# Another order of the projections in a two-layer hybrid decoder trunk, with later square roots and no forced wait for 1/rms

## The chip, the cores and the metric

One core of one Trainium2 chip runs the whole program. The metric is device microseconds from start to end of one execution. All arithmetic is at float32 precision: each product is formed by three matmuls on operands that are split into a rounded high part and a low rest (hi x hi, hi x lo, lo x hi). Weights stream from HBM once, 1 MB at a time, and are split on the chip.

## The reference

Two layers, 256 positions, width 1024. In each layer:

```
x = x + 0.5 * swiglu(rms_norm(x, ffn1_norm), w_gate, w_up, w_down)          # FFN 1, inner width 2816
h = rms_norm(x, mix_norm)
q, k, v, f, xr, gr, gA, gR = split(h @ w_in + b_in)                         # 1024 columns each, f has 8
q, k = rms_norm per head (8 heads of 128)
y_attn = softmax(q.k/sqrt(d) + c_t - c_s, causal) @ v, then @ w_o_attn      # c = cumsum(log_sigmoid(f))
xr = causal depthwise conv, width 4
r, i = sigmoid(block_diag(xr)), two gates
a = exp(-8 r softplus(-lam));  u = sqrt(1 - a^2) * i * xr;  hs_t = a_t hs_{t-1} + u_t
y_rnn = (hs * gelu(gr)) @ w_o_rnn
x = x + (sigmoid(gA) * y_attn + sigmoid(gR) * y_rnn) @ w_out
x = x + 0.5 * swiglu(rms_norm(x, ffn2_norm), ...)                           # FFN 2
```

## The kernel before

**A list of steps for TensorE.** The program is planned while it is built. `self.steps` is the fixed order of TensorE's work. A step is half of the product with one weight tile: 6 wide matmuls (512 columns, for q, k, v, whose output has positions on the partitions: `rows`) or 12 narrow ones (256 columns, for all others, whose output has channels on the partitions: `columns`). The mixer of a layer (`mix`, L685) begins at step `base`. Counted from there, before the change: q0 k0 v0 q1 k1 v1 are steps 0 to 47 (eight each; 0 and 1 are the first and the last four heads), xr 48 to 63, gr 64 to 79, gA 80 to 95, gR 96 to 111, then the output projections: attention ("ya") 112 to 127, recurrence ("yr") 128 to 143, and `w_out` 144 to 159. The host lays the weights out in the same order (`_weights`, L1164).

**Tasks for the other engines.** What follows a product is a Python generator (`projected`, `qk`, `head`, `recurrence`, `gated`, `stats`, ...). The planner keeps an own clock per engine (`Clock`, with a cost for each instruction, L75) and advances a task when the tile it names would be ready by that clock (`when`, `work`). Each advance puts instructions into the queues of TensorE (PE), ScalarE (ACT), VectorE (DVE), GpSimd (POOL) or SyncE (SP), which run them in order. A task can also hang on a condition of the plan (`must`). `need` advances tasks by force where a step must have their result. Tasks with the label "rnn" stand first in the list; heads and recurrences are background work, put off while ACT or DVE would be over 3.5 us (`ROOM`) ahead of PE by the planner's clock.

**Weights.** `split_half` turns one 128 x 1024 half of a loaded piece into hi (ACT cast) and lo (DVE subtraction). `run` (L397) does it 5 steps ahead at the latest (`LEAD`) and up to 20 (`AHEAD`) when ACT and DVE have room. Places are 8 W tiles, or R tiles while at least 8 of the 21 are idle. R tiles also hold q, k, v, the recurrence's and the gates' arrays.

**1/rms.** x is not normalised before a product. `stats` sums the squares by a matmul, takes the power on POOL, spreads the result over partitions by a second matmul on a diagonal (`sq`), and leaves it in `self.rb`. `projected` scales q, k, v as they leave PSUM; it gets the factor from `rms`, which forces `stats` on. `scaled` does the same for the columns, but waits for `self.rb`.

**Attention.** Four `head` tasks are spawned when k of their group is done; at most three are under way (`FLY`), in order.

**Recurrence.** `on_xr` spawns `recurrence` (L985) for each half of 512 channels: convolution on DVE (12 multiply-adds), gates by block-diagonal matmuls, tanh and exp on ACT, then a product under a root. The roots of both halves are taken together: Sqrt needs another ACT table than Exp, Tanh and Gelu. They wait until both halves have come so far and all heads are done or the step is over `base + 96`. After them come the scans, and `gated`: gelu (ACT, only once the roots are taken), product and split (DVE). yr reads that.

Of the kernel before, what the change touches and what calls it, by code (L numbers as in the profile page):

```python
# [33 lines left out]
OFF = {"q": 0, "k": 1024, "v": 2048, "f": 3072, "xr": 3080, "gr": 4104, "gA": 5128, "gR": 6152}  # L34
PROJ = [("q", 0), ("k", 0), ("v", 0), ("q", 1), ("k", 1), ("v", 1)]

P_G = {"ffn1": 0, "mix": 8, "ffn2": 16}
P_QN, P_KN, P_CW, P_CB, P_BA, P_BX, P_BGA, P_BGM, P_LAM, P_BXR, P_BGR, P_BV, NP_ = 24, 25, 26, 58, 66, 74, 82, 90, 98, 106, 114, 122, 130
LEAD = 5
# [9 lines left out]
AHEAD = 20  # L49
SLACK = 2.0  # L50
EARLYX = -0.4
SIDES = False

AT = 16, 48
# [7 lines left out]
class Clock:  # L62
# [12 lines left out]
    def cost(self, q, op, n, ins, kw):  # L75
        aps = sum(isinstance(kw.get(k), bass.AP) and kw[k].shape[-1] == 1 for k in ("scale", "bias", "scalar", "scalar1", "scalar2"))
        psum = ins and ins[0].space == bass.MemoryType.PSUM
        if q == "PE":
            two = ins[0].dtype == F32 and op == "matmul"
            return 2 * max(2 * n / 2400 + 0.003, 0.06) if two else max(n / 2330 + 0.007, 0.108)  # L80
        if q == "ACT":
            t = (0.051 if psum else 0.093) + 0.093 * (aps + (kw.get("accum_out") is not None)) + n / 1200
            need = self.TABLES.get(kw.get("func"))
            if need and self.table not in need:
                self.table = need[0]
                t += 1.3
            return t
        if q == "DVE":
            fast = op in ("tensor_scalar", "tensor_copy", "memset") and not psum
            return 0.068 + 0.061 * aps + n / (1920 if fast else 960)  # L90
        if q == "POOL":
            return 0.9 + n / 480
        return 0.0
# [103 lines left out]
class Trunk:  # L197
# [199 lines left out]
    def run(self):  # L397
        steps = self.steps
        first, last = {}, {}
        for s, st in enumerate(steps):  # L400
            first.setdefault(st.half, s)
            last[st.half] = s
        n = self.n_halves
        self.loaded, j = 3, 2
        self.first_halves()
        for s, st in enumerate(steps):
            self.s = s
            while j < n and first[j] - s <= LEAD and self.split_places():
                self.split_half(j)
                j += 1  # L410
            self.work()
            while (j < n and first[j] - s <= AHEAD and self.split_places()
                   and self.clock.done[self.raw[j // 2].tensor.name] <= self.now + EARLY
                   and all(self.clock.free[q] <= self.now + SLACK for q in ("ACT", "DVE"))):
                self.split_half(j)
                j += 1
            while st.half not in self.hl:
                if self.split_places():
                    self.split_half(j)
                    j += 1  # L420
                else:
                    self.push()
            hi, lo, places = self.hl[st.half]
            st.fn(hi, lo)
            if last[st.half] == s:
                places.give(hi, lo)
                del self.hl[st.half]
            for gen, label in st.done:
                self.spawn(gen, label)
        while self.tasks:  # L430
            self.push()
# [253 lines left out]
    def mix(self, l):  # L685
        base = len(self.steps)
        phase = self.phase
        self.phase += 1
        M = {"l": l, "p": self.prm_sb[:, l], "base": base, "phase": phase, "heads": 0}
        c = lambda t: slice(t * 128, (t + 1) * 128)  # L690

        def rows(i):

            nm, n = PROJ[i]
            js = [self.half() for _ in range(4)]
            self.spots.update(dict.fromkeys(js, (0, 0)))
            banks = {}

            def step(h, t):
                def fn(wh, wl):  # L700
                    if h == 0:
                        banks[t] = self.take(self.banks)
                    for kk in range(2):
                        k, w = 2 * h + kk, slice(kk * 512, (kk + 1) * 512)
                        xs = self.x_rhs(phase, k)
                        self.mm3(banks[t], xs[:, c(t)], xs[:, 256:512][:, c(t)], wh[:, w], wl[:, w], k == 0, k == 7)
                return Step(js[h], fn, [(self.projected(M, i, t, banks), "v" if nm == "v" else "qk")] if h == 3 else [])
            if i == 0:
                order = [(h, t) for t in range(2) for h in range(3)] + [(3, 0), (3, 1)]
            else:  # L710
                order = [(h, t) for h in range(4) for t in range(2)]
            self.steps += [step(h, t) for h, t in order]

        def columns(ds, rhs, done, late=False):

            banks = {}

            def step(d, half, ks):
                def fn(wh, wl):
                    if ks[0] == 0:  # L720
                        banks[d] = self.take(self.banks)
                    for k in ks:
                        w = slice(k * 128, k * 128 + 128)
                        self.product(banks[d], wh[:, w], wl[:, w], rhs(k), k == 0, k == 7)
                return Step(half, fn, [done(d, banks)] if ks[-1] == 7 else [])
            halves = {d: self.half() for d in ds}
            order = [(d, ks) for d in ds for ks in (range(4), range(4, 8))]
            if late:
                order[0:4] = [(d, ks) for d in ds[:2] for ks in (range(4), range(4, 7))] + [(d, range(7, 8)) for d in ds[:2]]
            self.steps += [step(d, halves[d], ks) for d, ks in order]  # L730

        def y_rhs(k):
            self.need(lambda: M["heads"] > k, "head", "qk", "forget", "v")
            return M["y", k // 2][1][:, k % 2]

        def r_rhs(k):
            self.need(lambda: ("yr", k // 2) in M, "rnn", "gr", "wd", "head")
            return M["yr", k // 2][1][:, k % 2]

        def m_rhs(k):  # L740
            self.need(lambda: ("m", k) in M, "ya", "merge", "gate")
            return M["mT", k // 2][1][:, k % 2]

        for i in range(6):
            rows(i)
        for nm, label, on in (("xr", "rnn", self.on_xr), ("gr", "gr", self.on_gr), ("gA", "gate", self.on_gate), ("gR", "gate", self.on_gate)):
            columns(range(8), lambda k: self.x_rhs(phase, k),
                    lambda d, b, nm=nm, label=label, on=on: (on(M, nm, d, b), label))
        self.starts.append((base - 14, lambda: self.prefetch(M), "bias"))
        self.starts.append((base - 12, lambda: self.block_diagonal(M), "wd"))  # L750
        self.starts.append((base + 8, lambda: self.forget(M), "forget"))
        columns(range(8), y_rhs, lambda d, b: (self.on_ya(M, d, b), "ya"))
        columns(range(8), r_rhs, lambda d, b: (self.on_yr(M, d, b), "merge"))
        columns(list(range(8)), m_rhs, lambda d, b: (self.on_out(M, d, b), "x"), late=True)
# [32 lines left out]

    def block_diagonal(self, M):
        for n in range(2):
            yield self.step_at(M["base"] + (40, 60)[n])  # L790
            raw, w = self.slot([4, 2, 128])
            self.SP.dma_start(out=w, in_=self.wbd[M["l"], n])
            yield self.when(raw, must=lambda: len(self.big.idle) >= 4)
            hi, lo = (self.slot([4, 2, 128], F32R, at) for at in AT)
            self.split(hi[1], lo[1], w)
            self.big.give(raw)
            M["wd", n] = hi, lo

    def projected(self, M, i, t, banks):

        nm, n = PROJ[i]
        bank, r = banks[t], self.rms(M["phase"])[:, t:t + 1]
        if nm == "v":
            if t == 0:
# [180 lines left out]
    def recurrence(self, M, n):  # L985
# [52 lines left out]
        if n == 0:  # L1038
            yield self.when(must=lambda: "roots" in M)
        else:  # L1040
            yield self.when(rt_t, must=lambda: ("rt", 0) in M and (M["heads"] == H or self.s > M["base"] + 96), queues=("ACT",))
            for i in range(2):
                self.ACT.activation(M["rt", i][0], M["rt", i][0], AF.Sqrt, scale=0.25)
            M["roots"] = True
# [119 lines left out]
def _weights(a):  # L1164
    out = []
    for l in range(L):
        w = a["w_in"][l]
        out += _ffn_halves(a["ffn1_w_gate"][l], a["ffn1_w_up"][l], a["ffn1_w_down"][l])
        out += [_rows(w[:, OFF[nm] + 512 * n:OFF[nm] + 512 * n + 512]) for nm, n in PROJ]
        out += [_columns(w[:, OFF[nm]:OFF[nm] + 1024]) for nm in ("xr", "gr", "gA", "gR")]  # L1170
        out += [_columns(a[nm][l]) for nm in ("w_o_attn", "w_o_rnn", "w_out")]
        out += _ffn_halves(a["ffn2_w_gate"][l], a["ffn2_w_up"][l], a["ffn2_w_down"][l])
    w = np.concatenate(out, axis=0)
# [43 lines left out]
```

## Time and profile before

| | |
|---|---|
| median of 3 runs | 1244.05 us (1242.8 to 1245.28) |
| profiled execution: time, span of the trace | 1245.86 us, 1244.1 us |
| PE busy | 1226.0 us, 99% of the span |
| PEld (weight loads of PE) busy | 1194.2 us, 96% |
| DVE busy | 851.8 us, 68% |
| ACT busy | 697.5 us, 56% |
| DMA, mean over the span | 187 GB/s, queue 1 busy 53.0% of 16 engines |
| mean granted TensorE clock | 0.995 |

Busy is time in which an engine has at least one instruction under way; ends of matmuls are modelled. The span runs from the first to the last instruction of the trace and is 1.76 us shorter than the profiled execution's time. All instructions carry line 154, that of the helper which records them, so groups go by tile names: `W` and `R` are the places above, `B` PSUM banks, `S` small tiles, `xs` the split x, `wr` loaded weights, `lg` and `pT` a head's logits and probabilities, `hb`, `prm`, `rst` parameters. In the trace the mixer of layer 0 runs from about 194 to 442 us and that of layer 1 from about 803 us to 1050.

### The profile page before, as it was taken

What the parts mean: (1) busy time and instruction counts of PE and PEld (TensorE: products, weight loads), DVE (VectorE), ACT (ScalarE), POOL (GpSimd) and SP (SyncE); (2) the same over time, 40 slices, a digit from 0 to 9 for tenths busy, and PEclk for the clock granted to TensorE, in tenths of its full rate; (3) what the DMA queues carried; (4) which work ended last, traced back from release to release, by engine and by line L of the source; (5) the groups of instructions that cost most, each with busy time, mean ns of one, the idle gap of its engine ahead of it and who ended that gap; (6) DMA issues with size and microseconds to landing.
All of it is one profiled execution on the core that took longest, in us unless ns stands there. A gap on an engine that the chain in (4) does not pass through costs nothing.

```text
span 1244.1 us, 24052 instructions
## 1 busy us (share of the span) xinstructions
PE 1226.0 (99%) x10040; PEld 1194.2 (96%) x10040; DVE 851.8 (68%) x1411; ACT 697.5 (56%) x1192; POOL 36.0 (3%) x48
## 2 busy tenths in 40 slices
PE   8999999999999999999999999999999899999998
PEld 7999998889999999999999999988999899999998
DVE  6765567678769976565675566776786599665552
ACT  6544446586795664444554445565658746544441
POOL 1000001120000000000000000011100000000000
PEclk9999999999999999999999999999999899999999
DMA  8655566543456755455575455663353557554451
GB/s 296 216 204 171 184 209 243 178 153 119 143 177 213 281 205 172 168 183 187 182 263 183 156 173 200 237 237 139 119 171 124 179 198 249 207 180 169 170 187 52
DMA packets 36029, 232.47 MB, mean 187 GB/s; under 512 B 4528, under 2 KB 5712, under 8 KB 9040
## 3 DMA queue, kind: packets, MB, share of 16 engines
q1 hardware_dynamic: 35776, 230.79, 53.0%
q8 instruction: 79, 1.29, 0.4%
q14 instruction: 30, 0.25, 0.1%
q10 hardware_dynamic: 144, 0.13, 0.0%
HBM read 229.84 MB, written 1.06 MB: 186 GB/s over the span
## 4 chain that ended last, share of the span: by engine, by line
PE 88%; DVE 6%; ACT 2%; DMA 2%; issue 1%; SPq 0%; ACTq 0%; DVEq 0%
PE B L154 88%; DVE R L154 3%; DVE W L154 2%; DMA wr<-ws 2%; ACT R L154 1%; ACT W L154 1%; DMA prm<-prm 0%; ACT L154 0%; SPq L154 0%; DVE acc L154 0%; DVE sq L154 0%; DVE x L154 0%; ACT sq L154 0%; ACT rb L154 0%; ACTq L154 0%
## 5 line engine op out<-in xcount | busy, mean ns | idle before, releaser
L154 DVE TENSOR_TENSOR W<-wr,W 128x1024 fp32r<-128x1024 f32 (+1 forms) x263 | 319.4, 1215 | 221.9 <-ACT W L154 220.4
L154 PE MATMUL B<-xs,W 128*128 128x256 f32 x3480 | 416.6, 279 | 7.1 <-ACT W L154 4.5
L154 PEld LDWEIGHTS B<-xs,W 128*128 128x128 f32 x3480 | 406.6, 189 | 10.0 <-ACT W L154 5.2
L154 ACT CAST W<-wr 128x1024 fp32r<-128x1024 f32 (+1 forms) x263 | 272.4, 1040 | 230.8 <-PE B L154 207.3
L154 PE MATMUL B<-R,W 128*128 128x256 f32 x2304 | 268.3, 277 | 4.3 <-DVE R L154 3.9
L154 PEld LDWEIGHTS B<-R,W 128*128 128x128 f32 x2304 | 265.2, 189 | 4.9 <-DVE R L154 4.3
L154 PE MATMUL B<-xs,R 128*128 128x256 f32 x2280 | 269.0, 277 | 0.0
L154 PEld LDWEIGHTS B<-xs,R 128*128 128x128 f32 x2280 | 263.2, 188 | 0.2
L154 DVE TENSOR_TENSOR R<-wr,R 128x1024 fp32r<-128x1024 f32 x163 | 197.6, 1220 | 66.2 <-ACT R L154 65.8
L154 ACT CAST R<-wr 128x1024 fp32r<-128x1024 f32 x163 | 166.3, 1040 | 3.3 <-DMA wr<-ws 3.2
L154 PE MATMUL B<-R,R 128*128 128x256 f32 (+1 forms) x1024 | 125.9, 279 | 0.0
L154 PEld LDWEIGHTS B<-R,R 128*128 128x128 f32 x1024 | 119.8, 188 | 0.6
L154 ACT ACTIVATE S<-S 128x256 f32<-128x256 f32 x88 | 36.3, 418 | 130.2 <-DVE S L154 130.2
L154 PE MATMUL B<-R,xs 128*128 128x512 f32 x336 | 84.1, 397 | 0.0
L154 PEld LDWEIGHTS B<-R,xs 128*128 128x128 f32 x336 | 61.6, 188 | 12.4
L154 PE MATMUL B<-W,xs 128*128 128x512 f32 x240 | 61.7, 398 | 0.0
L154 ACT CAST R<-S 128x256 fp32r<-128x256 f32 x88 | 34.9, 402 | 38.6 <-DVE S L154 38.6
L154 POOL TENSOR_TENSOR rst<-rst,mhalf 128x4 f32<-128x4 f32 (+1 forms) x22 | 27.2, 1239 | 954.0 <-DVE rst L154 954.0
L154 PEld LDWEIGHTS B<-W,xs 128*128 128x128 f32 x240 | 44.1, 188 | 8.7
L154 DVE TENSOR_TENSOR S<-B,S 128x256 f32<-128x256 f32 x88 | 36.4, 418 | 17.1 <-PE B L154 15.0
L154 DVE TENSOR_TENSOR R<-S,R 128x256 fp32r<-128x256 f32 x88 | 36.6, 420 | 15.2 <-ACT R L154 15.2
L154 ACT ACTIVATE xs<-x,prm 128x256 fp32r<-128x256 f32 x48 | 23.9, 506 | 23.9 <-DVE x L154 21.4
(116 smaller groups left out, 667.9 us busy)
## 6 DMA issues: line engine op xcount, KB each, us to landing
wr<-ws SPq DMA_DIRECT2D x210, 1024.0 KB, 4.8
bias<-b_in SPq DMA_DIRECT2D x8, 256.0 KB, 4.9
R<-cd SPq DMA_DIRECT2D x4, 512.0 KB, 4.9
R<-wbd SPq DMA_DIRECT2D x4, 512.0 KB, 5.7
x<-xT SPq DMA_DIRECT2D x4, 256.0 KB, 5.7
wr<-ws SPq DMA_DIRECT2D x4, 256.0 KB, 6.2
wr<-ws SPq DMA_DIRECT2D x2, 512.0 KB, 7.0
out<-x SPq DMA_DIRECT2D x8, 128.0 KB, 1.7
```

The lines of the kernel that those rows point to most:

```text
L154: return fn(*args, **kw)
```

## The change

The list of mixer projections becomes `MIX`: q0 k0 xr0 v0 xr1 q1 k1 v1 gr gA gR, eight steps each for the single ones (xr0 16 to 23, v0 24 to 31, xr1 32 to 39, q1 40 to 47, k1 48 to 55, v1 56 to 63; gr, gA, gR, ya, yr as before), and the weights lie in memory in that order. The block-diagonal weights are fetched and split from steps 8 and 36 on, not 40 and 60. The roots wait for all eight heads without the way out at `base + 96`. `projected` waits for 1/rms as `scaled` does, and no longer forces it. Near the end of a phase (a step that gives a new part of x within 3 steps behind or 2 ahead) weights are split at most 8 steps ahead, not 20. The planner's cost of a matmul falls from n/2330 + 0.007 to n/2259 (256 columns: 0.117 to 0.113 us).

```diff
+MIX = [('q',0),('k',0),('xr',0),('v',0),('xr',1),('q',1),('k',1),('v',1),('gr',0),('gr',1),('gA',0),('gA',1),('gR',0),('gR',1)]
...
+CALM = 2, 3
+NEAR = 8
...
-            return 2 * max(2 * n / 2400 + 0.003, 0.06) if two else max(n / 2330 + 0.007, 0.108)
+            return 2 * max(2 * n / 2400 + 0.003, 0.06) if two else max(n / 2259, 0.1)
...
-            while (j < n and first[j] - s <= AHEAD and self.split_places()
+            ends = any(lab == "x" for st in steps[max(0, s - CALM[1]):s + CALM[0]] for _, lab in st.done)
+            while (j < n and first[j] - s <= (NEAR if ends else AHEAD) and self.split_places()
...
-        for i in range(6):
-            rows(i)
-        for nm, label, on in (("xr", "rnn", self.on_xr), ("gr", "gr", self.on_gr), ("gA", "gate", self.on_gate), ("gR", "gate", self.on_gate)):
-            columns(range(8), lambda k: self.x_rhs(phase, k),
-                    lambda d, b, nm=nm, label=label, on=on: (on(M, nm, d, b), label))
+        on = {"xr": (self.on_xr, "rnn"), "gr": (self.on_gr, "gr"), "gA": (self.on_gate, "gate"), "gR": (self.on_gate, "gate")}
+        for nm, n in MIX:
+            if nm in "qkv":
+                rows(PROJ.index((nm, n)))
+            else:
+                columns(range(4 * n, 4 * n + 4), lambda k: self.x_rhs(phase, k),
+                        lambda d, b, nm=nm: (on[nm][0](M, nm, d, b), on[nm][1]))
...
-            yield self.step_at(M["base"] + (40, 60)[n])
+            yield self.step_at(M["base"] + 8 * MIX.index(("xr", n)) + (-8, 4)[n])
...
         nm, n = PROJ[i]
+        if M["phase"] not in self.rb:
+            yield self.when(must=lambda: M["phase"] in self.rb)
...
-            yield self.when(rt_t, must=lambda: ("rt", 0) in M and (M["heads"] == H or self.s > M["base"] + 96), queues=("ACT",))
+            yield self.when(rt_t, must=lambda: ("rt", 0) in M and M["heads"] == H, queues=("ACT",))
...
-        out += [_rows(w[:, OFF[nm] + 512 * n:OFF[nm] + 512 * n + 512]) for nm, n in PROJ]
-        out += [_columns(w[:, OFF[nm]:OFF[nm] + 1024]) for nm in ("xr", "gr", "gA", "gR")]
+        out += [(_rows if nm in "qkv" else _columns)(w[:, OFF[nm] + 512 * n:OFF[nm] + 512 * n + 512]) for nm, n in MIX]
```

## Rows read from the trace of the kernel before

**Rows 1.** The page's first part: busy time of each engine, its share of the span, and its instructions.

```profile
PE 1226.0 (99%) x10040; PEld 1194.2 (96%) x10040; DVE 851.8 (68%) x1411; ACT 697.5 (56%) x1192; POOL 36.0 (3%) x48
```

**Rows 2.** A quiet stretch, FFN 2 of layer 0 and FFN 1 of layer 1. Columns: stretch, its length, then busy time (and instructions) of PE, PEld, DVE, ACT, POOL, the mean granted clock, the DMA engines' busy share and GB/s.

```profile
447.00:805.00 358.00, 358.00 (x3148) 357.60 (x3148) 224.40 (x329) 174.94 (x251) 2.30 (x2) 1.00 0.55 191
```

**Rows 3.** The same view for stretches of the two mixers in which PE stops: the boundary into layer 0's mixer, layer 0's ya and yr, then layer 1's gR, its end, and the start of yr.

```profile
203.00:206.00 3.00, 2.04 (x9) 1.42 (x8) 2.62 (x5) 0.37 (x2) 0.00 (x0) 1.00 0.75 232
...
374.40:425.30 50.90, 49.02 (x430) 48.62 (x429) 50.38 (x74) 28.36 (x37) 0.00 (x0) 1.00 0.67 232
...
958.00:984.00 26.00, 22.41 (x173) 21.88 (x172) 15.71 (x20) 22.36 (x31) 0.00 (x0) 0.89 0.49 169
984.00:990.00 6.00, 6.00 (x50) 6.00 (x50) 2.15 (x4) 6.00 (x13) 0.00 (x0) 0.92 0.55 178
...
1010.00:1020.00 10.00, 7.59 (x53) 7.39 (x52) 9.89 (x15) 5.28 (x7) 0.00 (x0) 0.83 0.59 191
```

**Rows 4.** The timeline of PE in layer 1's mixer: start, length, engine, line, operation, output<-inputs, shape, count, and in brackets the idle time before and what ended it. `pT` is the last matmul of a head, `xs,W` from 950.21 on are the gates' steps, `R,W` from 990.03 on those of ya and yr.

```profile
946.72 0.88 PE L154 MATMUL B<-pT,R 128*128 128x256 f32 x4
...
948.16 1.54 PE L154 MATMUL B<-xs,W 128*128 128x256 f32 x12
...
950.21 24.80 PE L154 MATMUL B<-xs,W 128*128 128x256 f32 x216
978.00 0.67 PE L154 MATMUL B<-xs,W 128*128 128x256 f32 x2 [2.99 <-ACT W L154]
979.26 10.93 PE L154 MATMUL B<-xs,W 128*128 128x256 f32 x70 [0.59 <-DVE W L154]
990.03 22.04 PE L154 MATMUL B<-R,W 128*128 128x256 f32 x193
1014.48 12.71 PE L154 MATMUL B<-R,W 128*128 128x256 f32 x95 [2.41 <-DVE R L154]
```

**Rows 5.** The same view of layer 0's mixer: the last head of the first group and the end of the `rows` steps, the last head of all, the gates, ya and yr.

```profile
270.92 0.81 PE L154 MATMUL B<-pT,R 128*128 128x256 f32 x4
...
271.93 3.00 PE L154 MATMUL B<-W,xs 128*128 128x512 f32 x12
274.76 2.90 PE L154 MATMUL B<-xs,W 128*128 128x256 f32 x24
...
327.90 0.81 PE L154 MATMUL B<-pT,R 128*128 128x256 f32 x4
328.47 3.00 PE L154 MATMUL B<-xs,W 128*128 128x256 f32 x24
...
331.99 5.60 PE L154 MATMUL B<-xs,W 128*128 128x256 f32 x48
...
338.11 4.24 PE L154 MATMUL B<-xs,W 128*128 128x256 f32 x36
...
342.87 31.75 PE L154 MATMUL B<-xs,W 128*128 128x256 f32 x276
374.45 16.71 PE L154 MATMUL B<-R,W 128*128 128x256 f32 x146
391.55 13.66 PE L154 MATMUL B<-R,W 128*128 128x256 f32 x118 [0.39 <-DVE W L154]
...
425.27 0.86 PE L154 MATMUL B<-R,W 128*128 128x256 f32 x5 [1.50 <-DVE R L154]
```

**Rows 6.** The timeline of ACT where the roots are taken, layer 0 (first row) and layer 1. `R<-R 128x1024 x2` are the two square roots, `R<-R,hb` the tanh of a gate.

```profile
356.44 1.28 ACT L154 ACT_TABLE_LOAD   x1
...
971.50 1.28 ACT L154 ACT_TABLE_LOAD   x1 [2.80 <-DVE R L154]
972.80 2.01 ACT L154 ACTIVATE R<-R 128x1024 f32<-128x1024 f32 x2
974.81 1.28 ACT L154 ACT_TABLE_LOAD   x1
```

**Rows 7.** The timeline of all engines at the boundary into layer 0's mixer.

```profile
203.35 1.22 DVE L154 TENSOR_TENSOR R<-wr,R 128x1024 fp32r<-128x1024 f32 x1
...
205.02 0.70 PE L154 MATMUL B<-sq,ones 128*128 128x256 f32 x2 [0.96 <-DVE sq L154]
...
205.75 0.39 ACT L154 ACTIVATE rb<-B 128x256 f32<-128x256 f32 x1 [2.63 <-PE B L154]
```

**Rows 8.** DVE's groups from 815 to 1030 us, layer 1's mixer: busy time and mean ns of one. In this order: the convolution; the scans; the products after the roots (two with the root, two with the gelu); the products before them; the split of the block-diagonal matmuls' operand; the split of what yr reads.

```profile
L154 DVE SCALAR_TENSOR_TENSOR R<-R,prm,R 128x256 f32<-128x256 f32 x24 | 11.6, 482 | 0.6
...
L154 DVE TENSOR_TENSOR_SCAN R<-R,R 128x256 f32<-128x256 f32 x8 | 5.0, 672 | 0.0
L154 DVE TENSOR_TENSOR R<-R,R 128x1024 f32<-128x1024 f32 x4 | 4.9, 1213 | 0.0
L154 DVE SCALAR_TENSOR_TENSOR R<-R,R 128x1024 f32<-128x1024 f32 x4 | 4.8, 1221 | 0.0
...
L154 DVE TENSOR_TENSOR S<-R,S 128x256 fp32r<-128x256 f32 x8 | 3.4, 421 | 3.8 <-ACT S L154 3.8
...
L154 DVE TENSOR_TENSOR R<-R,R 128x512 fp32r<-128x512 f32 x4 | 2.6, 682 | 0.0
```

**Rows 9.** Busy times, as in rows 2, of layer 1's `rows` steps after k0.

```profile
837.00:883.50 46.50, 46.50 (x233) 39.02 (x232) 29.89 (x68) 30.11 (x85) 6.71 (x8) 1.00 0.43 151
```

**Rows 10.** The page's part on DMA issues, the block-diagonal weights: count, KB each, median us from issue to landing.

```profile
R<-wbd SPq DMA_DIRECT2D x4, 512.0 KB, 5.7
```

## The prediction

> **What bounds the kernel now.** I read the page's busy times first. PE is busy for 99% of the span, PEld for 96%, DVE and ACT for 68% and 56% [rows 1]: the kernel ends when PE has worked off its list, so only time in which PE stops or runs slowly can be won. In the FFNs there is none: over 358 us PE has no gap, at 358/3148 = 0.114 us a matmul, with DVE busy for 224 us [rows 2].
>
> So I looked, in the table of stretches, for those where PE's busy time is less than the stretch or the granted clock below 1. They lie in the mixers [rows 3]:
>
> - layer 1, gR (958 to 984): 26.00 - 22.41 = 3.59 us of stops. The mean clock there is 0.89, and 0.92 in the next 6 us: part of the time at 1.2 GHz, the rest at 2.4. A share missing from the clock is time missing: 0.11 x 26 + 0.08 x 6 = 3.3 us.
> - layer 1, start of yr (1010 to 1020): 2.41 us of stops, and 0.17 x 10 = 1.7 us by the clock of 0.83.
> - layer 0, ya and yr: 50.90 - 49.02 = 1.88 us, clock 1.00.
> - layer 0, boundary: 0.96 us, clock 1.00.
>
> Sum 3.59 + 3.3 + 2.41 + 1.7 + 1.88 + 0.96 = 13.8 us, 11.0 of them in layer 1. The clock fell after stops of 2.99 and 2.41 us and did not after one of 1.50 [rows 4, 5].
>
> What each stop waits for stands in the timelines. At 978.00 PE waits for an ACT cast of a weight half [rows 4]. ACT had stood idle for 2.80 us for DVE (the recurrence's operand of the root), then ran a table load, two roots and another load, 971.50 to 976.09, before it came to casts again [rows 6]. At 1014.48 and 425.27 PE waits for R from DVE, the last split that yr reads [rows 4, 5]: DVE is full there (50.38 of 50.90 us; 9.89 of 10) [rows 3], because scans, products and splits can only follow the roots. At 205.02 PE waits for `sq`, which DVE makes after a weight split of 1.22 us [rows 7]: `projected` forced the second stats matmul into PE's queue before its operand was there.
>
> **When the roots come, in steps.** From 342.87 to ya at step 112 lie 276 narrow matmuls, 23 steps, so 342.87 is step 89 and a step takes 31.6/23 = 1.37 us [rows 5]. Layer 0's roots, at 356.44, are 13.6/1.37 later: step 99 [rows 6]. In layer 1, 216 + 2 + 70 = 288 matmuls lie between 950.21 and ya, so 950.21 is step 88 [rows 4] and the roots at 971.50 [rows 6] are at 88 + 21.3/1.37 = step 103. The last heads end at step 89 - 108/12 = 80 (327.90) [rows 5] and 88 - 1 = 87 (946.72) [rows 4]. So before, heads were done first and the recurrence held the roots up; the way out at base + 96 did nothing in this trace.
>
> **The change part by part.**
>
> *xr earlier.* xr0 ends at step 24 instead of 56, xr1 at 40 instead of 64. The same matmuls and instructions run; nothing is added. The recurrences' DVE work ahead of the roots is 11.6 + 4.8 + 3.4 = 19.8 us a layer, after them 5.0 + 4.9 + 2.6 = 12.5 us [rows 8]. The first part moves into steps 24 to 64, some 57 us by PE's time. There DVE is busy for 29.89 of 46.5 us, 64%, and ACT for 65% [rows 9]: 0.64 x 57 + 19.8 = 56 us. It just fits, so the pre-root work should end at about step 64 to 70, not 99 and 103.
>
> *Heads later.* v1 ends at step 64 instead of 48, so now the heads decide when the roots come. Lower bound: a group of heads without a recurrence beside it. Layer 0's first group ends at 270.92, two wide steps ahead of 48 [rows 5]: step 46, 22 after v0 and 30 after k0. That gives 64 + 22 = 56 + 30 = step 86. Upper bound: the second group, which had both recurrences beside it, ended 80 - 48 = 32 and 87 - 48 = 39 steps after v1: steps 96 and 103. I take the lower half, 86 to 95, as the recurrence is past. Roots then come 4 to 17 steps (5 to 23 us) earlier than at 99 and 103. yr was late by 1.50 and 2.41 us, so its stops go: layer 1's 2.41 + 1.7. At the upper bound layer 1's stay.
>
> *The ACT jam.* When the roots come, their operand is long there, so ACT's 2.80 us of waiting goes; 4.6 us of loads and roots stay. The stop of 3.59 would shrink to 0.8 at most, and a shorter one than 1.50 did not lower the clock: 2.8 to 3.6 us and 3.3 us are won, even at the upper bound.
>
> *Roots wait for all heads.* Without the wait roots would now come before the heads' Exp and cost a further load each way, 2 x 1.28 us of ACT. Against before, no load is saved. The Trainium skill (ScalarE: Activation LUTs, What ACT_TABLE_LOAD costs) gives some 2.66 us for a switch, a drain of 1.38 us included, which would make it 5.3 us; here the roots begin 1.30 us after the load began [rows 6], so no drain is seen. What is queued behind the roots: scans, gelus and yr's splits; the way out is gone, so late heads are late yr.
>
> *q, k, v wait for 1/rms; fewer early splits at the ends.* This takes the forced matmul away; PE goes on with k0. The eviction of q0 comes after `rb`, at 206.1, some 1.1 us after the stop's end at 205.02 [rows 7]; q0 and k0 hold two PSUM banks each, stats and the forget logits one each: six of eight. So nothing should wait. Won: 0 to 0.96 us. The Trainium skill speaks against it (Perfetto Trace Analysis, Optimizing Tensor Performance, Matmuls): groups should rotate through banks so that evacuation overlaps the next group, and a held bank breaks that; if banks ran out, PE would stop until `rb`, about the 0.96 us it loses now. Splits 8 steps ahead rather than 20 still exceed the 5 that must be; if that cover fails, one stop like the 0.39 us for a W [rows 5] at each of five boundaries, 2 us lost.
>
> *Block-diagonal weights* at steps 8 and 36: two transfers of 512 KB a layer, 5.7 us to landing [rows 10], with DMA at 0.43 [rows 9] and the first use after step 24. Queued behind them on SP are weight pieces that are two ahead. Nothing; at worst one transfer's 5.7 us lateness eats lead.
>
> *R tiles.* Until the roots each recurrence holds four: eight of 21 for longer. Then weights are split into W tiles alone. The gates' 276 matmuls ran so without a gap [rows 5]: nothing.
>
> *The planner's matmul cost.* 0.113 instead of 0.117 us; the trace shows 0.114 with gaps between [rows 2]. It changes no instruction, only when things are queued. In the FFNs DVE's 37% of room hides it. Bounds: one stop of 0.39 us lost or won in each of four FFNs, 1.6 us.
>
> **Sum.** I take layer 1's 11.0 us as won, and let layer 0's 1.88 and 0.96 stand against small new stops that the rows can't show (2 + 1.6 us at the bounds above). The profiled execution took 1245.86 us, its span plus 1.76, and lies 1.81 above the median. 1245.86 - 11.0 = 1234.9 by its own time; with the 1.81, 1244.05 - 11.0 = 1233.0 for the median. All won: 1244.05 - 13.8 = 1230.2; with 1.6 from the planner 1228.6.
>
> **Rivals.**
>
> *Small gain.* The heads stay as slow as the second group was and end at steps 96 and 103. Then only the ACT jam goes, 2.8 + 3.3 = 6.1 us, and layer 0 gains up to 1.9: 1236 to 1238, up to 1241 with 3 us of new stops. For it: three at a time, in order, and the first group now has the recurrences beside it. Against: the second has not.
>
> *No change.* Stops move rather than go: PE waits for y at step 112 or for R tiles (eight recurrence, four y, three q1 k1 v1, two logit rows, two gr, two gA make 21 of 21 if heads end late). 1242 to 1246. Against: heads have 16 steps to spare even at step 96.
>
> *Slower.* Steps 24 to 64 are overfilled. 56 of 57 us counts as if DVE never waited; ACT is as full and each waits for the other. If the planner lets that work ahead of weight casts, PE stops for the excess. At an efficiency of 90% DVE needs 62 us: 5 us a layer, in stops over 2 us, each with 1.7 to 3.3 us by the clock. 2 x (5 + 2.5) = 15 lost against 11 to 13.8 won: 1245 to 1249. It decides from an excess of about 3.5 us a layer. For it: DVE was near full only where PE stopped [rows 3]. Against: heads and recurrences are background, which are put off by 3.5 us of lead.
>
> **How the numbers follow.** Forecast (1228.5 to 1236, likeliest 1233): 0.57. Small gain (1236 to 1241.5): 0.15. No change: 0.10. Slower: 0.18. Single runs of before lie within 0.1% of the median, so 0.2%, 2.5 us, is about what can be told: faster is under 1241.6, 0.72; same 0.10; slower 0.18. The range goes from 1229 to 1246: it takes in the first three and the mildest part of the last, and leaves out some 2 in 10.
>
> **What would show it.** Right: PE without a stop over 1 us and a clock of 1.00 in layer 1's gR, ya, yr; DVE clearly below 99% in ya and yr; roots at steps 86 to 95 without an idle wait ahead of the load; no `sq` stop at the boundaries. Wrong: PE waiting for W from DVE or ACT in steps 24 to 64, roots after step 103, a stop at the first y matmul, a clock below 1 in any mixer, or more than three table loads from roots to gelu.

## The result, and the profile after

The changed kernel takes 1227.63 us (median of 4 runs, 1227.54 to 1228.56) against 1244.44 us before (4 runs): the ratio is 0.9868, with an interval of 0.9851 to 0.9885. That is 16.8 us less. Forecast were 11.0 less and a range that ended at 1229: the direction is right, the size is not, and the time lies 1.4 us below the range.

The page of the changed kernel, busy times, and all that PE waits for in the whole execution:

```profile
span 1225.8 us, 24093 instructions
...
PE 1218.8 (99%) x10040; PEld 1190.1 (97%) x10040; DVE 844.4 (69%) x1387; ACT 698.6 (57%) x1214; POOL 38.9 (3%) x48
```

```profile
PE B L158 <- ACT W L158: 1.5, 1, 1.5
PE B L158 <- DVE mhalf L158: 1.1, 1, 1.1
PE B L158 <- ACT rb L158: 0.5, 1, 0.5
```

The share of PE is 99% as before [rows 1], with the same 10040 matmuls; 3.1 us of waits are left, all in the first 30 us. The next table cuts the changed kernel into stretches, in order: layer 0's mixer from its first wide matmul to ya; ya, yr and `w_out`; the FFNs between the mixers; the same two stretches of layer 1. Columns as in [rows 2].

```profile
190.33:370.31 179.98, 179.85 (x1258) 166.16 (x1257) 136.23 (x278) 132.29 (x294) 13.97 (x17) 1.00 0.48 169
370.31:435.59 65.28, 65.28 (x579) 65.28 (x578) 55.74 (x87) 36.81 (x54) 0.00 (x0) 1.00 0.58 210
435.59:796.50 360.91, 360.91 (x3182) 360.80 (x3181) 231.58 (x335) 179.41 (x257) 3.21 (x2) 1.00 0.56 196
796.50:975.74 179.24, 179.24 (x1257) 166.03 (x1256) 130.34 (x252) 133.62 (x296) 16.72 (x17) 1.00 0.49 170
975.74:1041.41 65.67, 65.60 (x578) 65.40 (x577) 57.86 (x92) 36.28 (x53) 0.00 (x0) 1.00 0.58 209
```

The same stretches of the kernel before, cut at its own marks:

```profile
193.84:374.45 180.61, 179.64 (x1257) 165.47 (x1256) 132.83 (x280) 129.08 (x282) 14.05 (x17) 1.00 0.48 169
374.45:442.28 67.83, 65.95 (x578) 65.55 (x577) 65.59 (x100) 41.66 (x60) 0.00 (x0) 1.00 0.66 235
442.28:803.20 360.92, 360.92 (x3182) 360.81 (x3181) 227.15 (x332) 177.11 (x254) 2.30 (x2) 1.00 0.55 190
803.20:990.02 186.82, 182.99 (x1257) 168.38 (x1256) 131.67 (x263) 130.23 (x283) 14.22 (x17) 0.98 0.47 165
990.02:1059.65 69.63, 67.22 (x578) 67.02 (x577) 65.69 (x98) 40.99 (x59) 0.00 (x0) 0.98 0.64 224
```

The difference of the two spans, 1244.1 - 1225.8 = 18.3 us, falls into place by these lengths: start and FFN 1 193.84 - 190.33 = 3.5; layer 0's projections 0.6; its ya to `w_out` 2.55; the FFNs 0.0; layer 1's projections 7.6; its ya to `w_out` 4.0. In the changed kernel no wait that the profile lists is left in the mixers, and the clock is 1.00 in all their stretches. DVE is 85% busy in layer 0's ya to `w_out` (55.74 of 65.28), where it was 97%.

The roots in the changed kernel, on ACT, and the last head and the gates' remaining steps on PE, layer 0 and layer 1:

```profile
345.50 1.28 ACT L158 ACT_TABLE_LOAD   x1
346.80 2.01 ACT L158 ACTIVATE R<-R 128x1024 f32<-128x1024 f32 x2
348.81 1.28 ACT L158 ACT_TABLE_LOAD   x1
350.11 1.71 ACT L158 ACTIVATE R<-R,prm 128x256 f32<-128x256 f32 x4
...
956.38 1.28 ACT L158 ACT_TABLE_LOAD   x1
957.68 2.01 ACT L158 ACTIVATE R<-R 128x1024 f32<-128x1024 f32 x2
```

```profile
343.78 0.81 PE L158 MATMUL B<-pT,R 128*128 128x256 f32 x4
344.35 26.12 PE L158 MATMUL B<-xs,W 128*128 128x256 f32 x228
370.31 1.86 PE L158 MATMUL B<-R,W 128*128 128x256 f32 x15
...
954.65 0.81 PE L158 MATMUL B<-pT,R 128*128 128x256 f32 x4
955.22 20.68 PE L158 MATMUL B<-xs,W 128*128 128x256 f32 x180
975.75 4.47 PE L158 MATMUL B<-R,W 128*128 128x256 f32 x38
```

The 2.80 us that ACT stood in front of the load [rows 6] are gone: no row has idle time in brackets. The last heads end 228/12 = 19 and 180/12 = 15 steps before step 112, at 93 and 97, and the roots follow within a step. The roots came at 99 and 103 before. Gelu follows the second load at once, so two loads lie between roots and gelu where there were three.

### The profile page after: what moved, and what is told of

Its sections match the earlier page's. It is cut to its first block, busy times and chain, and to the rows that moved or that the text cites. A ratio compares the mean times of both kernels' runs of the same rounds, so it can differ in the third digit from the quotient of the medians.

```text
span 1225.8 us, 24093 instructions
## 1 busy us (share of the span) xinstructions
PE 1218.8 (99%) x10040; PEld 1190.1 (97%) x10040; DVE 844.4 (69%) x1387; ACT 698.6 (57%) x1214; POOL 38.9 (3%) x48
## 4 chain that ended last, share of the span: by engine, by line
PE 95%; DVE 3%; DMA 1%; issue 1%; ACT 0%; SPq 0%; DVEq 0%; ACTq 0%
PE B L158 95%; DVE R L158 2%; DVE W L158 1%; DMA R<-cd 0%; DMA wr<-ws 0%; ACT W L158 0%; DVE lg L158 0%; DVE nm L158 0%; SPq L158 0%; DVE sq L158 0%; DVE S L158 0%; DVE x L158 0%; ACT rb L158 0%; ACT S L158 0%; ACT dp L158 0%
## 5 line engine op out<-in xcount | busy, mean ns | idle before, releaser
L158 DVE TENSOR_TENSOR W<-wr,W 128x1024 fp32r<-128x1024 f32 (+1 forms) x293 | 355.0, 1214 | 176.6 <-ACT W L158 176.0
L158 PE MATMUL B<-xs,W 128*128 128x256 f32 x3768 | 449.0, 278 | 1.9 <-ACT W L158 1.5
L158 PEld LDWEIGHTS B<-xs,W 128*128 128x128 f32 x3768 | 437.5, 188 | 3.5 <-ACT W L158 1.8
L158 ACT CAST W<-wr 128x1024 fp32r<-128x1024 f32 (+1 forms) x293 | 302.0, 1039 | 167.8 <-PE B L158 133.9
L158 PE MATMUL B<-xs,R 128*128 128x256 f32 x1992 | 235.3, 276 | 0.0
L158 PEld LDWEIGHTS B<-xs,R 128*128 128x128 f32 x1992 | 230.3, 188 | 0.2
L158 DVE TENSOR_TENSOR R<-wr,R 128x1024 fp32r<-128x1024 f32 x133 | 160.9, 1219 | 37.4 <-ACT R L158 37.4
L158 PE MATMUL B<-W,xs 128*128 128x512 f32 x444 | 106.5, 393 | 0.0
L158 PEld LDWEIGHTS B<-W,xs 128*128 128x128 f32 x444 | 82.4, 188 | 16.7
L158 DVE TENSOR_TENSOR S<-B,rb 128x256 f32<-128x256 f32 x88 | 36.3, 417 | 0.0
```

Source lines behind the costliest of these rows:

```text
L158: return fn(*args, **kw)
```

## The experiments

Theory, as it stood after the result: the order carries the mixers' 13.8 us; what exceeds it is the start, where the trace is 3.5 us shorter and where the planner's matmul cost alone differs. Rivals: the planner's cost or the calm ends cure the mixers; the start is luck. Each median stands beside that of the kernel before which was measured together with it.

**The planner's cost alone, throughout** (kernel before)

```diff
-            ... max(n / 2330 + 0.007, 0.108)
+            ... max(n / 2259, 0.1)
```

> The kernel before with the planner's new matmul cost alone (n/2259). Theory 'planner at the start': the copy of 1/rms leaves ACT's queue ahead of a weight cast that waits for its transfer, so PE stops at most 0.6 us near 30 us and the clock stays at 2.4 GHz there: 3 to 4 us won, 1240.5 to 1241.5, with the mixers' stops about as before. Rival 'luck of the first transfers': the first 42 us differ by when the weights landed in that execution, and the time stays at 1244 +- 1. Rival 'the planner's cost cures the mixers too': layer 1's jam of 3.59 us and its clock loss go, 1236 or less.

1245.89 us against 1243.82 (ratio 1.0017, 1.0008 to 1.0027): slightly slower, which neither the theory nor a rival had foreseen. Its start is short, but yr is late:

```profile
PE B L154 <- ACT R L154: 5.7, 1, 5.7
PE B L154 <- DVE R L154: 4.6, 2, 3.7
```

Layer 1's jam at gR is gone from the list, and in its place layer 0's yr waits 5.7 us for the split of the last R; layer 1's yr waits 3.7 us, where it was 2.4. The cost reorders the queues everywhere; with the old order it is no gain.

**The planner's cost at the start alone** (kernel before)

```diff
+            ... max(n / 2259, 0.1) if self.free["PE"] < 40 else max(n / 2330 + 0.007, 0.108)
```

> The kernel before with the new matmul cost only while the planner's PE time is under 40 us, the old one after that. Theory 'planner at the start': the same 3 to 4 us as the new cost throughout, 1240.5 to 1241.5, start without a clock of 1.2 GHz near 32 us, mixers as before (layer 1's stops of 3.59 and 2.41 us still there). Rival 'luck of the first transfers': 1244 +- 1.

1243.19 us against 1243.82 (0.9992, 0.9983 to 1.0001): 0.6 us, not told from none; 3 to 4 us is refuted. Most of the 3.5 us between the two profiled starts therefore belongs to those executions and not to the change (last section).

**The order alone** (kernel before)

```diff
+MIX = [('q',0),('k',0),('xr',0),('v',0),('xr',1),('q',1),('k',1),('v',1),('gr',0), ...]
...
+            yield self.step_at(M["base"] + 8 * MIX.index(("xr", n)) + (-8, 4)[n])
```

> The kernel before with the new order of the projections alone (and the block-diagonal weights fetched for it); old matmul cost, roots with the way out, forced 1/rms, early splits as before. Theory 'the order carries the mixers': layer 1's two stops and its clock loss go, 11.0 us, and layer 0's 1.88: 1231 to 1234, start and boundary stop (0.96 us) as before. Rival 'the order needs the better planner': with the old cost new stops for W appear in the mixers, 1236 to 1242. If the way out matters, the roots come at step 97 in front of the last heads and Exp's table is loaded once more.

1233.89 us against 1243.82 (0.9922, 0.9906 to 0.9939): 9.9 us won. The mixers' waits for yr and the jam are gone. The three longest groups of waits that are left are these, and the one for `W` and 0.7 of the 1.9 us for `sq` lie in the start:

```profile
PE B L155 <- DVE sq L155: 1.9, 3, 1.0
PE B L155 <- ACT W L155: 1.6, 1, 1.6
PE B L155 <- DVE f L155: 1.5, 1, 1.5
```

The order is the main cause: the four stretches of the mixers are together 9.7 us shorter than before, from the first wide matmuls (191.61 and 800.29) to the ends of `w_out` (439.37 and 1047.72). The other 1.2 us for `sq` are the stops at the two boundaries, 0.96 and 0.25 us. The order also opens a new stop: the matmul that sums up the forget gates (`f`) waits 1.46 us at 827.78, in layer 1, where the kernel before had none.

**All but the order** (changed kernel, old order of the projections)

```diff
-MIX = [('q',0),('k',0),('xr',0),('v',0),('xr',1),('q',1),('k',1),('v',1), ...]
+MIX = [('q',0),('k',0),('v',0),('q',1),('k',1),('v',1),('xr',0),('xr',1), ...]
...
-            yield self.step_at(M["base"] + 8 * MIX.index(("xr", n)) + (-8, 4)[n])
+            yield self.step_at(M["base"] + (40, 60)[n])
```

> The changed kernel with the old order of the projections and the old fetching steps (40 and 60) of the block-diagonal weights: all other parts of the change are in. Theory 'the order carries the mixers': only the start's 3.5 us and the boundary's about 1 us are won against before, 1238 to 1241. Rival 'the planner or the calm ends cure the mixers': 1234 or less.

1252.28 us against 1243.82 (1.0065, 1.005 to 1.008): 8.5 us slower. Both theories missed that. PE in layer 0, and ACT, which makes the split that PE waits for:

```profile
369.32 0.81 PE L158 MATMUL B<-pT,R 128*128 128x256 f32 x4
...
402.25 7.95 PE L158 MATMUL B<-R,W 128*128 128x256 f32 x39 [9.59 <-ACT R L158]
```

```profile
370.96 1.28 ACT L158 ACT_TABLE_LOAD   x1
...
401.58 1.14 ACT L158 CAST R<-R 128x512 fp32r<-128x512 f32 x2 [10.66 <-DVE R L158]
```

This is what the prediction called late heads being late yr: the last head's last matmuls run from 369.32, the table load of the roots starts at 370.96, and 402.25 - 370.96 = 31.3 us pass before yr goes on. The stop of 9.59 us and the slower clock after it follow. Roots at step 112 are not the whole of its cause, as the next run shows.

**The same with the way out** (old order, all else changed, roots as before)

```diff
-            ... ("rt", 0) in M and M["heads"] == H
+            ... ("rt", 0) in M and (M["heads"] == H or self.s > M["base"] + 96)
```

> Old order with all other parts of the change, but with the roots' way out at base + 96 restored; without it this came to 1252.3. There the last head ended at step 112 in layer 0 and the roots came at once after it. Theory 'the wait for all heads is what costs in the old order': roots at about step 105, yr's stop of 9.6 us in layer 0 shrinks by most of it: 1242 to 1246. Rival 'the recurrence itself is late there (its last tanh and its product stand right ahead of the roots)': 1250 to 1254.

1246.66 us against 1244.79 (1.0012, 1.0003 to 1.0022): between the two expectations, and 1.9 us above the kernel before where the run without the way out was 8.5 above it. So the wait for all heads costs some 6 us in the old order (5.6 by the two medians, 6.6 by their distances from the kernel before). The roots did not come earlier, at 371.65, for their operand was late too; but the last head came behind them, and in layer 0 PE stops for y instead of yr, for less:

```profile
372.76 0.81 PE L158 MATMUL B<-pT,R 128*128 128x256 f32 x4
378.11 33.62 PE L158 MATMUL B<-R,W 128*128 128x256 f32 x267 [4.53 <-ACT R L158]
```

Layer 0's yr has its operand in time here, with roots 0.7 us later than without the way out: DVE takes up the first product behind the roots at 379.80, where it was 387.46. What counts for yr is thus also how soon DVE comes to the work behind the roots. Layer 1's stop for yr stays as it was, 6.84 us against 6.85. So in the old order heads and recurrence were both late, and what either waits for decides where PE stops and for how long. Which of the other parts of the change makes them late there was not tested.

**The way out in the new order** (changed kernel, the edit above)

> The changed kernel with the roots' way out at base + 96 restored. In the changed kernel the last head ends at step 93 in layer 0 and 97 in layer 1. Theory 'all heads are in time': nothing changes in layer 0, in layer 1 the roots come a step or so earlier with a further load of 1.28 us on ACT at most, hidden: 1227.6 +- 0.7. Rival 'the wait for all heads carries a part of the gain': 1229 or more.

1227.86 us (0.9866, 0.9851 to 0.9881): no difference. In the order of this change the wait for all heads does nothing that the times show.

**The old matmul cost in the changed kernel**

```diff
-            ... max(n / 2259, 0.1)
+            ... max(n / 2330 + 0.007, 0.108)
```

> The changed kernel with the planner's old matmul cost (n/2330 + 0.007); order, roots, 1/rms and calm ends as changed. Theory 'order first, the rest at the boundaries': the mixers keep their gain, the copy of 1/rms stands behind a cast at the start again (about 1 us): 1228 to 1231. Rival 'the cost is what takes order alone (1233.9) to 1227.6': 1232 to 1235.

1231.55 us (0.9896, 0.9881 to 0.9911), above the end of the first range and below the start of the second. Against 1227.86 of the run beside it, the cost is worth 3.7 us here. That is the middle of two values: the four runs lie in two pairs, 1230.3 and 1230.5, 1232.6 and 1232.9, which are 2.5 and 4.9 us above the run beside them. The profiled one is of the slower pair and has the clock at half speed near 33 us. In that trace the start to the first wide matmul of the mixer is 194.5 us long, 4.2 us more than in the changed kernel, and ya to `w_out` of layer 0 66.1 us against 65.3; the four stretches of the mixers are together 1.2 us longer.

**The old cost at the start alone** (changed kernel)

```diff
+            ... max(n / 2330 + 0.007, 0.108) if self.free["PE"] < 40 else max(n / 2259, 0.1)
```

> The changed kernel with the planner's old matmul cost only while its PE time is under 40 us, the new one after that. Before it, the new cost at the start alone won 0.6 us (interval -0.1 to 2.1) on the kernel before, and the old cost throughout lost 3.9 us on the changed one. Theory 'the start is worth about what the stops and the clock there show': the copy of 1/rms stands behind a cast again, some 1.2 us of stops, and in part of the executions a fall of the clock near 33 us (1.7 us): 1228.5 to 1230.5, in two clusters. Rival 'the start is worth nothing, old cost loses in ya and yr': 1227.6 +- 0.5.

1229.13 us (1228.28 to 1229.5; 0.9874, 0.9859 to 0.9888), against 1227.62 (1227.21 to 1228.07) of the run with more warm matmuls beside it, which is the changed kernel but for those: by these medians the start is worth 1.5 us, with 0.2 us between the two ranges, and the two clusters that were expected did not come. A single trace can't carry that value: to the first wide matmul this kernel took 191.25 us, the changed one 190.33, and the changed one with the way out, whose program is the same up to there, 191.50. The mechanism shows in two rows of ACT and one of PE; first this kernel, then the changed one:

```profile
29.24 1.04 ACT L158 CAST W<-wr 128x1024 fp32r<-128x1024 f32 x1 [1.15 <-DMA wr<-ws]
30.19 0.38 ACT L158 ACTIVATE rb<-B 128x256 f32<-128x256 f32 x1
...
30.62 3.04 PE L158 MATMUL B<-xs,W 128*128 128x256 f32 x24 [0.98 <-ACT rb L158]
```

```profile
29.28 0.38 ACT L158 ACTIVATE rb<-B 128x256 f32<-128x256 f32 x1 [0.72 <-PE B L158]
29.64 1.05 ACT L158 CAST W<-wr 128x1024 fp32r<-128x1024 f32 x1
...
29.72 4.49 PE L158 MATMUL B<-xs,W 128*128 128x256 f32 x37 [0.47 <-ACT rb L158]
```

With the old cost the copy of 1/rms (`rb`) is queued on ACT behind a cast that waits 1.15 us for its transfer; with the new one it goes first. PE's matmul (`B<-xs,W`) does not read `rb`; by the kernel's text, what it waits for there is the PSUM bank that this copy reads and so frees.

**1/rms forced again** (changed kernel)

```diff
-        if M["phase"] not in self.rb:
-            yield self.when(must=lambda: M["phase"] in self.rb)
```

> The changed kernel with the eviction of q, k, v forcing 1/rms again, as before. Theory 'the forced matmul stops PE at the boundaries': stops of 0.5 to 1.6 us near 201 and 810 us as in the order alone, 2 to 4 us in all: 1229.5 to 1231.5. Rival 'calm ends have made the operand early enough': 1227.6 +- 0.7.

1232.52 us (0.9905, 0.9888 to 0.9921), 4.7 us more than the 1227.86 beside it: more than was expected.

```profile
PE B L158 <- DVE sq L158: 2.4, 2, 1.2
PE B L158 <- ACT W L158: 2.2, 1, 2.2
PE B L158 <- DVE mhalf L158: 1.1, 1, 1.1
PE B L158 <- DVE R L158: 0.7, 2, 0.5
```

Two stops of 1.2 us are the forced matmul at the two boundaries, as at 205.02 before [rows 7]. The mixers' stretches are longer by more than these, by 4.5 us. Part of the rest is that layer 0's heads and so its yr come later: the last head's last matmuls run from 355.92 instead of 343.78, there are 0.7 us of waits for R, and ya to `w_out` takes 66.6 instead of 65.3 us. What makes layer 1's projections 0.8 us longer than their stop explains stays open.

**Early splits everywhere** (changed kernel without the limit)

```diff
-            while (j < n and first[j] - s <= (NEAR if ends else AHEAD) and ...
+            while (j < n and first[j] - s <= AHEAD and ...
```

> The changed kernel without the limit of 8 steps near the end of a phase: weights are split up to 20 steps ahead everywhere, as before. Theory 'calm ends matter at the boundaries': stops at the two boundaries into the mixers return in part, 1 to 2 us: 1228.5 to 1230. Rival 'the wait for 1/rms alone does it': 1227.6 +- 0.7.

1229.08 us (0.9876, 0.9861 to 0.989), 1.2 us more than the 1227.86 beside it, with the ranges apart. But the stop is at another boundary than expected, from FFN 2 of layer 0 into FFN 1 of layer 1, where PE waits for a new part of x:

```profile
622.88 0.86 PE L158 MATMUL B<-xs,R 128*128 128x256 f32 x5 [0.74 <-DVE xs L158]
```

**More warm matmuls** (changed kernel)

```diff
-WARM = 9
+WARM = 13
```

> The changed kernel with 13 instead of 9 warm matmuls ahead of the first product: nothing else. In the traces the clock at the start rises between 5 and 14 us and in part of them falls again once, since PE stands idle from about 5.3 to 6.7 us. Theory 'the start can still be bettered': the pause closes, the clock comes earlier or does not fall again, 1 to 2 us: 1225.5 to 1227. Rival 'the first weights set the start': 1227.6 +- 0.5, or a little later if the matmuls delay the first product.

1227.62 us (0.9863, 0.9848 to 0.9877): no gain. The warm matmuls now last from 1.12 to 7.04 us, and the pause ahead of the first product shrinks from 1.45 to 0.20 us, but that product comes at 7.23 instead of 6.78. From 7.23 to 14.00 us PE has 48 matmuls in either kernel, so no gain by the shorter pause shows, and the later begin stays: 190.74 instead of 190.33 us to the first wide matmul.

No version that was tried beats the changed kernel by more than the runs can tell. Not tried were the wait for 1/rms or the calm ends alone on the kernel before.

## Why the prediction was right in its mechanism and wrong in size

**What bounds the kernel.** Right: PE's list sets the end, and the gain is the time in which it stopped or ran slowly. With no stop left in the mixers the kernel ends at the length of that list.

**The mixers' terms.** Nearly right in size, and in place but for one stop. Layer 1: 11.0 forecast, 7.58 + 3.96 = 11.5 measured. Layer 0 with its boundary: 1.88 + 0.96 = 2.8 shown by the rows, 0.6 + 2.55 = 3.2 measured. Of these 14.7 us the order alone gave 9.7 in its trace; undone in the changed kernel, the wait for 1/rms gives back 4.5 of them and the planner's cost 1.2.

Two readings behind these terms were wrong. Layer 0's stop of 1.50 us at 425.27 is not yr's. From the start of ya to this stop lie 427 matmuls, 2 x 192 of ya and yr and 43 of `w_out`; PE waits there for the last operand of `w_out`, whose split DVE makes only after three weight splits:

```profile
421.39 3.49 DVE L154 TENSOR_TENSOR R<-wr,R 128x1024 fp32r<-128x1024 f32 x3
424.80 0.42 DVE L154 TENSOR_TENSOR R<-R,R 128x256 fp32r<-128x256 f32 x1
```

So earlier roots were no reason by themselves for this stop to go. It is gone with the order alone, though; what lets DVE get there in time stays open. And that a stop shorter than 1.50 us did not lower the clock holds for the mixers only: in the same trace it was lower near 33 us, after stops of 0.53 and 1.14 us (last section).

**Heads and roots.** Last heads at steps 93 and 97, in the bounds of 86 and 103, layer 1 a little over the half that I took. The bounds held and the point mattered little, as yr had room at either: its last split ends some 10 us ahead of its first matmul in layer 0 and 4.5 us in layer 1. The work ahead of the roots was to end at step 64 to 70; by the count of matmuls it ended near 80 and 82 (DVE's last product at 319.71 and 928.53), which was still ahead of the last heads. That no load is saved was wrong: one in each layer is, since gelu now comes right behind the roots; no stop hung on it.

**The step that failed: the sum.** I let layer 0's 2.8 us stand against "small new stops that the rows can't show". There were none in the changed kernel, and no row of the trace had spoken for them: a term that the rows carry was struck out against one that they don't. With the order alone there is one, the 1.46 us for `f`; the other parts took it away. 13.8 instead of 11.0 would have given 1230.2.

**The term that was mis-sized: the planner's matmul cost.** I called it 0 with bounds of 0.39 us for each FFN. At the start alone it is worth 1.5 us by the medians (old cost at the start alone), by the order of two instructions on ACT. I had looked for stops in the mixers only, though the trace of before had PE wait near 30 us too. With the old cost throughout the loss is 3.7 us in the new order (2.5 or 4.9 by the pairs), more than the 1.6 us of all its bounds together, while in the old order the new cost loses 2.1. It is no small term with a sign of its own: it redraws all queues.

Mixers 11.5 + 3.2 and start 1.5 make 16.2 of the 16.8 us, the mixers by one trace each and the start by medians.

**The wait for 1/rms and the calm ends.** This term was mis-sized too. Won were to be 0 to 0.96 us; undone, it costs 4.7, part of it by later heads. Whether the old order needs it less was not tested. Fewer early splits were priced only as a possible loss; undone, they cost 1.2 us. The rule of the Trainium skill on rotating PSUM banks (Perfetto Trace Analysis, Optimizing Tensor Performance, Matmuls) brought no stop in the mixers. The trace agrees with it in the first FFN, where evacuation also waits for 1/rms: the 0.47 us that PE waits for `rb` at 29.72 are, by the kernel, a wait for a bank.

**The rivals.** "Small gain" and "no change" did not come. "Slower" rested on steps 24 to 64 being overfilled, 56 of 57 us of DVE. From xr0 to the end of v1, steps 16 to 63, layer 0 of the changed kernel shows:

```profile
215.91:295.27 79.36, 79.23 (x487) 70.52 (x486) 64.92 (x138) 60.95 (x156) 10.78 (x12) 1.00 0.49 175
```

64.92 of 79.36 us is 82%. The estimate took some 1.4 us a step and left out the matmuls of heads and gates that run among them: 48 steps take 79 us, not 66 to 68. Late heads as the price of the wait for all of them is real, but in the old order.

**What was to show it.** All came true but two: no stop over 1 us and a clock of 1.00 in the mixers, no idle ahead of the load, no `sq` stop, two loads. The roots in layer 1 lie at step 97 rather than in 86 to 95. And DVE is clearly below 99% in ya and yr of layer 0 only, 94%; in layer 1 it is still 98.5% busy:

```profile
370.31:413.83 43.52, 43.52 (x387) 43.52 (x386) 40.86 (x59) 26.32 (x35) 0.00 (x0) 1.00 0.68 242
975.74:1019.30 43.56, 43.56 (x387) 43.56 (x386) 42.91 (x64) 25.57 (x34) 0.00 (x0) 1.00 0.67 242
```

So a full DVE is not by itself what stops PE there. What changed is that the last of yr's splits now ends 4.5 us before yr needs it.

## What to carry to other kernels

Where one engine is full, add up its stops over the whole trace, the first microseconds too, and strike none against losses that no row shows. Count the instructions up to a stop before saying which product it belongs to. Work that many things wait for belongs early in the list of the full engine, and the gain is known from the stops that wait for it. The edits of a planner are not additive: one that wins some 4 us in one order loses 2 in another, so each has to be timed with the others in place.

## What the runs showed of the hardware

A stop near 30 us is followed by a lower clock in some traces and not in others. Two kernels, both with the old matmul cost and both with the new order: the kernel before with the order alone changed, and then the changed kernel with the old cost throughout.

```profile
32.00:38.00 6.00, 6.00 (x55) 6.00 (x54) 4.46 (x12) 4.11 (x9) 0.00 (x0) 1.00 0.65 223
```

```profile
32.00:38.00 6.00, 5.70 (x35) 5.70 (x36) 4.46 (x9) 3.03 (x8) 0.00 (x0) 0.72 0.71 236
```

In the first PE issues 55 matmuls in 6 us at a granted clock of 1.00, in the second 35 at 0.72, part of it at 1.2 GHz. Ahead of it both stop for the same two things, `sq` and `rb`: 0.72 and 0.70 us in the first, 0.70 and 0.93 in the second. The second also stops for weights four times between 7 and 16 us, 0.23 to 0.56 us each, where the first does so once, for 0.23. Whether these differences decide, or the execution, stays open. For the execution speak the four runs of the second kernel: their mean granted clocks are 0.999 and 0.997 in the slower pair and 1.000 in both of the faster, 2.3 us apart, with one and the same program. Only one of them has a trace.

The profiled execution of the kernel before had the lower clock there as well:

```profile
32.00:38.00 6.00, 6.00 (x40) 6.00 (x40) 4.46 (x11) 3.47 (x8) 0.00 (x0) 0.72 0.61 206
```

Its start, up to the first wide matmul, and that of the changed kernel:

```profile
0.00:193.84 193.84, 188.62 (x1608) 186.59 (x1609) 127.82 (x195) 102.46 (x153) 3.84 (x11) 0.99 0.61 213
0.00:190.33 190.33, 187.26 (x1608) 186.01 (x1609) 125.93 (x193) 99.73 (x151) 3.36 (x11) 1.00 0.61 218
```

Of the 3.5 us between them 5.22 - 3.07 = 2.15 are time in which PE stood still and 1.36 a longer busy time with the same 1608 matmuls, while the change to the start is worth 1.5 by medians. One profiled execution is not enough to price a term of that size.
